# Score products of 64 inputs over all 128 rows, in a two-block transformer on one NeuronCore

## The chip, the cores and the metric

The kernel runs on one core of one Trainium2 chip. The metric is the device time of one execution in microseconds (us). Five engines work side by side: TensorE (PE in the profile, with its weight loads as PEld), VectorE (DVE), ScalarE (ACT), GpSimd (POOL) and SyncE (SP), which mostly issues transfers. Three runs of the kernel before took 2697.49, 2701.44 and 2704.54 us; the median is 2701.44 us.

## The reference, cut to what matters

A first block of two layers works on 512 tokens and a context of 256 tokens, all of width 1024. Each layer modulates and norms its input, projects it, and feeds three mixers: a pooling, a neighbourhood attention of 6 heads, and a bidirectional retention of 6 heads. An output projection and a convolutional FFN follow. A second block (latent attention, a long convolution, a memory attention and 32 experts) comes behind; the change doesn't touch it. All heads of the first block have 64 features, so each score is a sum over 64 inputs:

```python
# neighborhood_attention: each query against a window of 8 rows x 32 columns and 256 context tokens
s_loc = jnp.einsum('bnqhd,binshd->bhnqis', qb, kb)
s_loc = jnp.where(valid, s_loc + bias, NEG_INF)
s_ctx = jnp.einsum('bnqhd,bkhd->bhnqk', qb, kc)
p = jax.nn.softmax(jnp.concatenate([s_loc, s_ctx], axis=-1), axis=-1)
# retention: q and k rotated; the scores times decays instead of a softmax
a = jnp.einsum('bhid,bhjd->bhij', qb, kb) * intra[None]
y = a @ v + (q @ state_of_the_context) * q_dec
```

## The kernel before, in words

**Products.** Every float32 operand is split into two float32r parts, hi and lo, whose sum is exact. A product of 128 inputs (`mm3`) is three matmuls: hi by hi, lo by hi, hi by lo. A score product of 64 inputs (`mm2`) is two. For this, two heads share a tile of 128 partitions, 64 each. One operand (the keys in the attention, the queries in the retention) is stacked: for each head a tile with its hi part in the head's own 64 rows and its lo part in the other 64. The other operand is doubled: its hi part stands on both halves of a tile of each head (`qd`, `rkd`), so the first matmul, over all 128 rows, gives hi by hi and hi by lo. Its lo part stands in one tile for both heads (`ql`, `cql`, `rkl`), and the second matmul takes only the head's own 64 rows of it, `mm(out, xl, ks[r])`.

**Neighbourhood attention** (phase `na_l` of layer l, `neighborhood`). The three pairs of heads come one after the other. A unit is one head's block of 128 queries: 24 units in each layer, and 6 more in layer 0 for the context's own queries (`na_context`). A unit has three stages: scores and softmax, transpose of the probabilities, product with the values. `staged` keeps three units in flight, one stage apart, and the projections of the next pair (`lin`) are woven between them. A unit makes two score products of 256 columns, so two first and two second matmuls.

**Retention** (phase `ret_l`, `ret_pair`), also a pair at a time. The queries are rotated (`rotated`: a shuffled copy `sw`, times a table on POOL, added on DVE), stacked, and multiplied by a decay for either direction (`dq(d)`: an iota on POOL, an exponential on ACT, then a product on POOL into `x`, which is split). The keys are rotated and doubled. `sw`, `x` and the square of the group norm share one buffer, `rsw`; the decays take two, `rd`; the decayed context keys have one, `rckd`. Then each head's blocks of 128 keys go against all 512 queries (four first and four second matmuls for each head, 512 columns wide; in layer 0 the context's 2 blocks as well, 256 columns wide). The scores are multiplied by the decays on DVE, split on ACT and DVE, and multiplied by the values.

A tile scheduler orders the instructions of each engine from the program's order and its own estimates, and a buffer that is asked for again waits until its last reader is done.

Of the kernel before, what the change touches and what calls it, by code (L numbers as in the profile page):

```python
# [11 lines left out]
F32 = mybir.dt.float32  # L12
FR = mybir.dt.float32r
# [5 lines left out]
P = 128  # L19
D = 1024  # L20
KC = D // P
S = 512
# [4 lines left out]
# the FFN's features go through the chip in parts: chunks of 128 in each  # L27
FF = (8, 7, 7)
# adding and taking off MAGIC rounds to the nearest integer
MAGIC = 1.5 * 2.0 ** 23  # L30
# 2 pi in three parts, the first two short enough for exact products with small integers
# [3 lines left out]
# the slots of a tile of an expert's tokens, and the tiles: one for each of the 32 experts, and the  # L35
# most that more tokens than that can take (each 64 of 1024), with one to spare
CAP = 64
# thirds of experts' weights in flight: in memory that gets free before the last linear layer, before
# the routing, and after it
# [3 lines left out]
# the early ones, by the chunk of that layer that they are asked for after  # L43
EARLY = (0, 0, 1, 1, 2, 1, 2, 2)
# experts whose tokens are in flight
GATHERED = 8
# The order of the steps of the four long convolutions (of the first and the second, halves of the channels
# each), and of the output projections of the latent attention and of the hyena.
ON_VECTOR = {(1, 0, 1), (2, 0, 2), (0, 0, 0), (1, 0, 0), (3, 1, 2), (1, 0, 2), (0, 0, 1), (1, 1, 1)}
CONV = "a a a * b a b * * a a a b * a b a * b c c b b b * c b c * d d c c * c d * c d c d d d d d + +".split()  # L50
# The order of the steps that the kernel starts with: of the memory, the filters, the modulation, the stream's loads and
# its norm; and of those left
# [3 lines left out]
# added to the half rows of free slots: beyond the last of the tokens' and the results'  # L56
FREE = 4 * S * 4
# PSUM's banks, by use: linear layers, scores, transposes and statistics, sums over scores, and what
# goes on beside
BANKS = {"lin": 2, "sc": 2, "pt": 2, "o": 1, "bg": 1}  # L60
SL = ((0, S), (S, T))
# the parts that a layer's tokens are taken in where a norm follows: tokens, sequence
SEGS = (((0, S, 0), (S, T, 1)), ((0, C, 0), (C, S, 0)))

# Vectors that the chip takes with their features on the partitions: name, columns.
# [12 lines left out]
# The retention's decays, one column for every pair of heads (64 rows each), and one for each head.  # L78
# [4 lines left out]
def whole(steps):  # L83
    """A generator's result, all its steps taken."""
    while True:
        try:
            next(steps)
        except StopIteration as e:
            return e.value


def weave(main, beside, slots, steps):
    """Both generators' steps: of beside's as large a part as of main's."""
    done = 0
    for i, _ in enumerate(main, 1):
        while done * slots < i * steps:
            next(beside, None)
            done += 1
    whole(beside)
# [6 lines left out]
class Builder:  # L106
    def __init__(self, ctx, tc, a, out):
# [7 lines left out]
        self.opened = {}  # L115
        self.np, self.nw, self.ahead = None, S, 2
        self.turn = True
# [37 lines left out]
    def norms(self, name, width=S, ahead=2, side="right"):  # L155
        """Opens the memory of the norms to come, of no more tokens than width, ahead chunks at a time."""
        self.nw, self.ahead = width, ahead
        self.np, self.np_name = self.open(name, side), name

    def normed(self):  # L160
        """Closes what norms opened."""
# [10 lines left out]

    def weight(self, src, n, pool=None):
        """n columns of 128 rows, split into two float32r parts whose sum is exact."""
# [10 lines left out]
    def exact(self, src):  # L185
        """1024 columns of a constant that comes with its second float32r part."""
# [15 lines left out]
    def doubled(self, tag, n, bufs=2):  # L202
        """Memory for the first operand of mm2: of a pair of heads."""
        return [self.t([P, n], FR, f"{tag}d{i}", bufs) for i in range(2)], self.t([P, n], FR, tag + "l", bufs)

    def split_doubled(self, hd, lo, src, at=lambda t: t):
        """Two heads' src in two parts: the first twice, on both halves of the partitions of a tile of each head."""
        nc = self.nc
        for i in range(2):
            r, o = slice(64 * i, 64 * i + 64), slice(64 - 64 * i, 128 - 64 * i)  # L210
            nc.scalar.copy(at(hd[i][r]), src[r])
            nc.vector.tensor_tensor(out=at(lo[r]), in0=src[r], in1=at(hd[i][r]), op=ALU.subtract)
            nc.scalar.copy(at(hd[i][o]), src[r])  # L213

    def split_stacked(self, out, src, scale):
        """Two heads' src times scale in two parts, on the halves of the partitions of a tile of each head: the
        first in its place, the second on the other half."""
# [7 lines left out]
    def mm2(self, out, xd, xl, ks, r):  # L225
        """mm3 for 64 inputs: a first part on all partitions with both parts at once."""
        mm = self.nc.tensor.matmul
        mm(out, xd, ks, start=True, stop=False)
        mm(out, xl, ks[r], start=False, stop=True)

    def linear_steps(self, w, xh, xl, sl, m=P, ps=None):
        """psum[features, tokens] of one tile of m output features; a step for each 128 inputs."""
# [14 lines left out]
    def linear_turn(self, w, xh, xl, sl):  # L247
        """linear where the scores' banks are free too."""
# [3 lines left out]
    def split(self, hi, lo, src, scale=1.0):  # L252
        """src times a power of two, into two float32r parts."""
# [13 lines left out]
    def rstd(self, acc, count, ones=None):  # L267
        """Of every token, 1 / sqrt(the sum over acc's partitions / count + eps), on each partition. With ones
        [128, m]: of m blocks of partitions."""
# [7 lines left out]
    def tokenwise(self, acc, ones=None):  # L277
        """Memory for something of every token, with the tokens on the partitions: [128, n / 128, m]; and the
        sums over acc's partitions, or over blocks of them."""
# [9 lines left out]
    def spread(self, r, n, bufs=1):  # L289
        """[128 tokens, n / 128, m] -> [128, n], the same on each of m blocks of partitions"""  # L290
# [12 lines left out]
    def add_square(self, acc, ch, first, scale=1.0, tag="sq"):  # L303
        """Adds the square of ch times scale to acc."""
# [8 lines left out]
    def normed_steps(self, h, sl, acc, scale, shift, ah, al):  # L313
        """rmsnorm of h's tokens sl, whose squares' sums by partition are acc, times scale(k) plus shift(k),
        in two parts; a step for the rstd and for each chunk."""
# [11 lines left out]
    def affine_split(self, hi, lo, x, scale, shift=None):  # L327
        """x times the features' scale, plus their shift, in two parts."""
# [20 lines left out]

    def setup(self):  # L350
# [17 lines left out]
        # (norm, layer) -> g * (1 + scale)  # L368
        self.gs = {(l, i): self.const(f"gs{l}{i}", [P, KC, 2]) for l in range(DEPTH) for i in (1, 2)}

    def stream(self):
        """A chunk of features of the residual stream, or of what the mixers return."""
# [5 lines left out]
    def acts(self):  # L378
        """The two parts of 1024 features."""
# [5 lines left out]
    def modulation(self, l, r):  # L385
        """Columns 2048 r to 2048 (r + 1) of silu(c) @ w_mod[l] + b_mod[l], for x and the context."""
# [30 lines left out]
    def modulation_rows(self, l, r, seqs):  # L417
        """The same by products over rows, off the tensor engine, for the sequences seqs. A step for each 128."""
# [27 lines left out]
    def beside(self, *steps):  # L446
        """What goes on beside the rest: a piece at every tick."""
# [18 lines left out]

    def mod_scale(self, l, i, s):
        """The scale and the shift of norm i for sequence s."""
# [3 lines left out]
    def softmax(self, sc, bias=None, groups=1):  # L472
        """Softmax of sc [128 queries, groups * n keys] over the keys of each group."""
# [4 lines left out]
        pr = self.t([P, 512], F32, "pr", 2)[:, :w]  # L478
        sign = 1.0
        if bias is not None:  # L480
            u = self.t([P, 512], F32, "su", 2)[:, :w]
            nc.vector.tensor_tensor_reduce(out=u, in0=sc, in1=bias, scale=-1.0, scalar=3.0e38,
                                           op0=ALU.add, op1=ALU.min, accum_out=small[:, 0:1])
            sc, sign = u, -1.0
# [14 lines left out]
    def transposed(self, pr, ph, pl):  # L499
        """The transpose of pr [128 queries, w keys] in two parts, to ph, pl [128 keys, w / 128, 128 queries]."""  # L500
# [1829 lines left out]
```

## Time and profile before

| | |
|---|---|
| median of 3 runs | 2701.44 us |
| span of the profiled execution | 2694.9 us |
| time outside the span, by the median | 6.5 us |
| neighbourhood attention, layer 0 | 195 to 345 us of the span |
| retention, layer 0 | 345 to 540 us |
| neighbourhood attention, layer 1 | 1211 to 1338 us |
| retention, layer 1 | 1338 to 1506 us |

The span runs from the first to the last instruction of the one profiled execution; the run's time is a few microseconds longer. The four stretches are those in which the changed lines work, 640 us of the span together.

### The profile page before, as it was taken

Reading aid. Unit: us, or ns where it says so; the run is one execution under the profiler, and the core shown is the slowest. Engines: PE = TensorE matmul, PEld = TensorE weight load, DVE = VectorE, ACT = ScalarE, POOL = GpSimd, SP = SyncE. Lnnn points to the kernel's source line nnn. Section 1 sums busy time; section 2 is a strip of 40 time slices with the busy share of each in tenths; the row PEclk is TensorE's granted clock in tenths of the full one; section 3 lists DMA queues with packets and bytes.
Section 4 is the critical chain, followed back from the end, with each engine's and each line's share of the span. In section 5 each row is a group of like instructions: output and inputs, shape, how many; then the busy total and the mean of one; then the engine's idle time right before and its main releaser. Section 6 shows DMA issues by size and latency. Waiting matters only on the chain. (4 is left out here: it accounts for less than half of the span.)

```text
span 2694.9 us, 37557 instructions
## 1 busy us (share of the span) xinstructions
PE 2561.7 (95%) x14286; PEld 2014.3 (75%) x14286; DVE 1713.9 (64%) x2932; ACT 1171.5 (43%) x1971; POOL 421.2 (16%) x432
## 2 busy tenths in 40 slices
PE   7999999999999999989999999999999879989996
PEld 5567767788888888877766888888878768845553
DVE  6656666557667666476666664546788986355554
ACT  6544445655313313354455652434666545311102
POOL 3041111120000000142221200001500540121100
PEclk9999999999999999999999999999999989989998
DMA  7741222152334252252111522233311643689980
GB/s 242 274 153 48 83 87 94 64 162 93 95 121 159 93 187 85 76 170 58 51 40 40 174 94 94 94 102 111 109 63 63 213 135 108 233 309 365 379 324 32
DMA packets 114047, 368.90 MB, mean 137 GB/s; under 512 B 17988, under 2 KB 29648, under 8 KB 101450
## 3 DMA queue, kind: packets, MB, share of 16 engines
q1 hardware_dynamic: 110554, 358.10, 38.6%
q0 software_dynamic: 3312, 8.40, 0.9%
q8 instruction: 113, 1.85, 0.3%
q14 instruction: 68, 0.56, 0.1%
HBM read 356.95 MB, written 13.68 MB: 138 GB/s over the span
## 5 line engine op out<-in xcount | busy, mean ns | idle before, releaser
L198 PE MATMUL lin<-ah,whi 128*128 128x512 f32 (+1 forms) x1504 | 562.4, 374 | 14.3 <-ACT qd L213 9.3
L200 PE MATMUL lin<-al,whi 128*128 128x512 f32 (+1 forms) x1504 | 547.5, 365 | 1.7 <-DVE al L332 1.1
L199 PE MATMUL lin<-ah,wlo 128*128 128x512 f32 (+1 forms) x1504 | 546.1, 364 | 2.8 <-DVE wlo L182 2.8
L181 ACT CAST whi<-wraw 128x1024 fp32r<-128x1024 f32 (+2 forms) x297 | 297.2, 1004 | 305.1 <-PE sc L200 171.0
L182 DVE TENSOR_TENSOR wlo<-wraw,whi 128x1024 fp32r<-128x1024 f32 (+2 forms) x297 | 370.9, 1250 | 91.6 <-ACT whi L181 91.0
L198 PEld LDWEIGHTS lin<-ah,whi 128*128 128x128 f32 x1504 | 286.5, 191 | 70.7 <-ACT qd L213 9.7
L200 PEld LDWEIGHTS lin<-al,whi 128*128 128x128 f32 x1504 | 285.6, 190 | 50.1 <-DVE al L332 2.4
L199 PEld LDWEIGHTS lin<-ah,wlo 128*128 128x128 f32 x1504 | 286.8, 191 | 42.5 <-DVE wlo L182 3.3
L311 POOL TENSOR_TENSOR sqacc<-sqacc,sq 128x256 f32<-128x256 f32 (+1 forms) x101 | 127.3, 1266 | 1087.8 <-ACT sq L310 1086.5
L198 PE MATMUL sc<-ah,whi 128*128 128x256 f32 (+1 forms) x696 | 219.5, 316 | 0.9 <-ACT whi L181 0.9
L199 PE MATMUL sc<-ah,wlo 128*128 128x256 f32 (+1 forms) x696 | 219.1, 315 | 0.0
L200 PE MATMUL sc<-al,whi 128*128 128x256 f32 (+1 forms) x696 | 218.5, 315 | 0.1
L198 PEld LDWEIGHTS sc<-ah,whi 128*128 128x128 f32 x696 | 132.5, 190 | 12.0 <-ACT whi L181 1.1
L199 PEld LDWEIGHTS sc<-ah,wlo 128*128 128x128 f32 x696 | 132.5, 190 | 10.1 <-DVE wlo L182 0.2
L200 PEld LDWEIGHTS sc<-al,whi 128*128 128x128 f32 x696 | 132.2, 190 | 8.4 <-DVE al L257 0.3
L877 DVE SCALAR_TENSOR_TENSOR fv<-lin,vec,fv 128x511 f32<-128x511 f32 x67 | 50.1, 748 | 118.6 <-ACT fv L876 118.5
L1908 PE MATMUL lin<-ew,ex 128*64 128x256 f32 x864 | 116.7, 388 | 0.0
L433 DVE CUSTOM_DVE_ANT_0 mraw<-mraw,crow 128x512 f32<-128x512 f32 x128 | 86.8, 689 | 32.2 <-DMA mraw<-in_w_mod_rows 31.0
L199 PE MATMUL lin<-mh,wlo 128*128 128x512 f32 (+1 forms) x292 | 105.3, 361 | 1.6 <-DVE wlo L182 1.4
L198 PE MATMUL lin<-mh,whi 128*128 128x512 f32 (+1 forms) x292 | 105.3, 361 | 0.0
L200 PE MATMUL lin<-ml,whi 128*128 128x512 f32 (+1 forms) x292 | 104.8, 359 | 0.0
L1908 PEld LDWEIGHTS lin<-ew,ex 128*64 128x64 f32 x864 | 65.7, 138 | 47.0 <-issue 19.6
(633 smaller groups left out, 5339.7 us busy)
## 6 DMA issues: line engine op xcount, KB each, us to landing
ew<-in_w_moe SPq DMA_DIRECT2D x81, 1024.0 KB
wraw<-in_w_up SPq DMA_DIRECT2D x88, 512.0 KB
wraw<-in_w_in SPq DMA_DIRECT2D x61, 512.0 KB
mraw<-in_w_mod SPq DMA_DIRECT2D x48, 512.0 KB
mraw<-in_w_mod_rows SPq DMA_DIRECT2D x96, 256.0 KB
wraw<-in_w_down SPq DMA_DIRECT2D x48, 448.0 KB
wraw<-in_w_out SPq DMA_DIRECT2D x32, 512.0 KB
wraw<-in_w_down SPq DMA_DIRECT2D x16, 512.0 KB
```

The lines of the kernel that those rows point to most:

```text
L181: nc.scalar.copy(hi[:, :n], raw[:, :n])
L182: nc.vector.tensor_tensor(out=lo[:, :n], in0=raw[:, :n], in1=hi[:, :n], op=ALU.subtract)
L198: mm(out, wh, xh, start=start, stop=False)
L199: mm(out, wl, xh, start=False, stop=False)
L200: mm(out, wh, xl, start=False, stop=stop)
L311: nc.gpsimd.tensor_tensor(out=acc, in0=acc, in1=sq, op=ALU.add)
L433: self.tc.keep_in_program_order(nc.vector.tensor_tensor_reduce(out=x, in0=raw, in1=self.crow[:, i, d], scale=1.0, scalar=0.0, op0=ALU.mult ...
L877: nc.vector.scalar_tensor_tensor(out=v[:, t0 + 1:t1], in0=ps[:, :t1 - t0 - 1], scalar=cw(0), in1=v[:, t0 + 1:t1], op0=ALU.mult, op1=ALU.add)
L1908: nc.tensor.matmul(ps[CAP * f:CAP * f + CAP, :256], xk, pieces(512 * k + 256 * f, 256), start=k == 0, stop=k == KC - 1, tile_position=(0, ...
```

## The change

It has three parts. First, the doubled operand's lo part gets a tile for each head, whose other 64 rows are set to zero once a phase, by 16 memsets on POOL in all; the second matmul of `mm2` then runs over all 128 rows, against the whole stacked tile. Second, the softmax of scores with a bias writes biased scores into the buffer of the probabilities, of which there are three in the neighbourhood attention, instead of into a buffer `su` of their own (there were two of each). Third, in the retention `sw`, `x`, the decayed context keys and the square all take the two `rd` buffers, the decays being multiplied in place; `rsw` and `rckd` are gone.

```diff
     def doubled(self, tag, n, bufs=2):
-        return [self.t([P, n], FR, f"{tag}d{i}", bufs) for i in range(2)], self.t([P, n], FR, tag + "l", bufs)
+        key = tag, self.sm.name
+        if key not in self.seconds:
+            self.seconds[key] = []
+            for _ in range(bufs):
+                pair = [self.t([P, n], FR, tag + "l", 2 * bufs) for _ in range(2)]
+                for i, t in enumerate(pair):
+                    self.nc.gpsimd.memset(t[64 - 64 * i:128 - 64 * i].bitcast(F32), 0.0)
+                self.seconds[key].append(pair)
+        lo = self.seconds[key].pop(0)
+        self.seconds[key].append(lo)
+        return [self.t([P, n], FR, f"{tag}d{i}", bufs) for i in range(2)], lo
...
     def split_doubled(self, hd, lo, src, at=lambda t: t):
-            nc.vector.tensor_tensor(out=at(lo[r]), in0=src[r], in1=at(hd[i][r]), op=ALU.subtract)
+            nc.vector.tensor_tensor(out=at(lo[i][r]), in0=src[r], in1=at(hd[i][r]), op=ALU.subtract)
...
-    def mm2(self, out, xd, xl, ks, r):
+    def mm2(self, out, xd, xl, ks):
         mm(out, xd, ks, start=True, stop=False)
-        mm(out, xl, ks[r], start=False, stop=True)
+        mm(out, xl, ks, start=False, stop=True)
...
     def softmax(self, sc, bias=None, groups=1):
-        pr = self.t([P, 512], F32, "pr", 2)[:, :w]
+        pr = self.t([P, 512], F32, "pr", self.probs)[:, :w]
         if bias is not None:
-            u = self.t([P, 512], F32, "su", 2)[:, :w]
-            nc.vector.tensor_tensor_reduce(out=u, in0=sc, in1=bias, scale=-1.0, scalar=3.0e38,
+            nc.vector.tensor_tensor_reduce(out=pr, in0=sc, in1=bias, scale=-1.0, scalar=3.0e38,
-            sc, sign = u, -1.0
+            sc, sign = pr, -1.0
...
     def rotated(self, x):
-        sw = self.t([P, S], F32, "rsw", 1)
+        sw = self.t([P, S], F32, "rd", 2)
...
-            x = self.t([P, S], F32, "rsw", 1)
-            nc.gpsimd.tensor_tensor(out=x, in0=q, in1=dq(d), op=ALU.mult)
+            x = dq(d)
+            nc.gpsimd.tensor_tensor(out=x, in0=q, in1=x, op=ALU.mult)
...
-            kd = self.t([P, C], F32, "rckd", 1)
-            nc.vector.tensor_tensor(out=kd, in0=ck, in1=dk(d), op=ALU.mult)
+            kd = dk(d)
+            nc.vector.tensor_tensor(out=kd, in0=ck, in1=kd, op=ALU.mult)
...
-            sq = self.t([P, S], F32, "rsw", 1)[:, :n]
+            sq = self.t([P, S], F32, "rd", 2)[:, :n]
```

In `layer`, `self.probs` is 3 during the neighbourhood attention and 2 elsewhere. No matmul is added or removed, and PE's order in the neighbourhood attention is the same but for one block. Two places show what moves.

POOL, where the neighbourhood attention of layer 0 begins, before. L838 is the last step of the pooling, `bias` is what is added to the scores of a pair, `vw` a window of the values.

```order
L838 TENSOR_TENSOR hy_1478<-hy_1478,px_1459 128x256
L562 MEMSET bias_1717 128x2x256
L562 MEMSET bias_1798 128x2x256
L844 MEMSET poolw_2348 128x256
L567 TENSOR_TENSOR bias_1717<-bias_1717,namask_1506 128x256 x2
L567 TENSOR_TENSOR bias_1798<-bias_1798,namask_1506 128x256 x2
L570 COPY vw_1729<-vf_1651 128x256
```

The same place of the changed kernel:

```order
L848 TENSOR_TENSOR hy_1478<-hy_1478,px_1459 128x256
L211 MEMSET ql_1567 64x512
L211 MEMSET ql_1568 64x512
L211 MEMSET ql_1571 64x512
L211 MEMSET ql_1572 64x512
L211 MEMSET cql_1583 64x256
L211 MEMSET cql_1584 64x256
L211 MEMSET cql_1587 64x256
L211 MEMSET cql_1588 64x256
L573 MEMSET bias_1731 128x2x256
L573 MEMSET bias_1810 128x2x256
L854 MEMSET poolw_2352 128x256
```

Eight memsets of half a tile stand ahead of the first two biases; layer 1 has four there, and each retention two.

DVE, in the first pair of the retention of layer 0, before. L257 is the second part of a split (here of the decayed queries `rqd0` and `rqd1`), L684 to L687 are the rotation of the keys, L212 the keys' lo part.

```order
L257 TENSOR_TENSOR rqd0l_3532<-rsw_3526,rqd0h_3531 128x512
L737 TENSOR_TENSOR rckd_3704<-rck_3605,rd_3705 128x256
L182 TENSOR_TENSOR wlo_4070<-wraw_4068,whi_4069 128x1024
L257 TENSOR_TENSOR rqd1l_3541<-rsw_3535,rqd1h_3540 128x512
L212 TENSOR_TENSOR rkl_3602<-rck_3605,rkd_3600 64x256
L684 STREAM_SHUFFLE rsw_3667<-rx_3603 128x512
L212 TENSOR_TENSOR rkl_3602<-rck_3605,rkd_3601 64x256
L686 TENSOR_TENSOR rx_3603<-rx_3603,rope_3488 128x512
L687 TENSOR_TENSOR rx_3603<-rx_3603,rsw_3667 128x512
L212 TENSOR_TENSOR rkl_3602<-rx_3603,rkd_3600 64x512
L212 TENSOR_TENSOR rkl_3602<-rx_3603,rkd_3601 64x512
```

The same place of the changed kernel:

```order
L269 TENSOR_TENSOR rqd0l_3517<-rd_3512,rqd0h_3516 128x512
L695 STREAM_SHUFFLE rd_3654<-rx_3590 128x512
L697 TENSOR_TENSOR rx_3590<-rx_3590,rope_3474 128x512
L182 TENSOR_TENSOR wlo_4055<-wraw_4053,whi_4054 128x1024
L269 TENSOR_TENSOR rqd1l_3525<-rd_3520,rqd1h_3524 128x512
L698 TENSOR_TENSOR rx_3590<-rx_3590,rd_3654 128x512
L223 TENSOR_TENSOR rkl_3584<-rck_3592,rkd_3588 64x256
L223 TENSOR_TENSOR rkl_3585<-rck_3592,rkd_3589 64x256
L748 TENSOR_TENSOR rd_3691<-rck_3592,rd_3691 128x256
L223 TENSOR_TENSOR rkl_3584<-rx_3590,rkd_3588 64x512
L223 TENSOR_TENSOR rkl_3585<-rx_3590,rkd_3589 64x512
```

The shuffle of the keys stood behind the split of the second direction, whose buffer it takes; it now stands right behind the split of the first.

## Rows read from the trace of the kernel before

**Rows 1.** The page: the profiled execution's span.
```profile
span 2694.9 us, 37557 instructions
```

**Rows 2.** Windows: length, busy us (count) of PE, PEld, DVE, ACT, POOL; clock; DMA.
```profile
195.00:345.00 150.00, 148.63 (x982) 114.66 (x981) 93.88 (x220) 67.89 (x155) 22.40 (x40) 1.00 0.23 72
345.00:540.00 195.00, 189.66 (x1001) 135.48 (x999) 124.22 (x214) 113.64 (x196) 31.98 (x36) 0.97 0.24 84
1211.00:1338.00 127.00, 123.76 (x823) 99.03 (x823) 80.22 (x183) 59.78 (x123) 24.32 (x37) 1.00 0.18 50
1338.00:1506.00 168.00, 156.05 (x801) 118.86 (x800) 117.87 (x177) 93.15 (x154) 39.28 (x45) 0.97 0.17 58
1358.00:1369.00 11.00, 9.59 (x24) 5.27 (x24) 6.38 (x12) 6.66 (x12) 0.56 (x1) 0.53 0.00 0
371.50:382.20 10.70, 10.70 (x28) 5.55 (x27) 4.86 (x10) 5.96 (x11) 0.56 (x1) 0.52 0.29 98
```

**Rows 3.** One line, L229, the second matmul: count, ns min/median/max, starts, forms.
```profile
L229 PE MATMUL sc<-k,ql x96: 377/382/386, 198.9 to 1330.7; 64*128 64x256 f32 x96
L229 PE MATMUL sc<-rq,rkl x60: 378/497/793, 371.7 to 1482.8; 64*128 64x512 f32 x48, 64*128 64x256 f32 x12
L229 PE MATMUL sc<-k,cql x12: 379/380/382, 235.9 to 339.9; 64*128 64x256 f32 x12
```

**Rows 4.** Timeline of PE around one unit's scores, layer 0: start, us, instruction.
```profile
211.00 0.28 PE L228 MATMUL sc<-k,qd 128*128 128x256 f32 x1
211.21 0.38 PE L229 MATMUL sc<-k,ql 64*128 64x256 f32 x1
211.52 0.38 PE L228 MATMUL sc<-k,qd 128*128 128x256 f32 x1
211.84 0.38 PE L229 MATMUL sc<-k,ql 64*128 64x256 f32 x1
212.14 0.38 PE L198 MATMUL lin<-ah,whi 128*128 128x256 f32 x1
212.37 0.28 PE L199 MATMUL lin<-ah,wlo 128*128 128x256 f32 x1
```

**Rows 5.** Timeline of PE in a projection, 256 columns, five pitches apart.
```profile
1353.66 0.28 PE L200 MATMUL lin<-al,whi 128*128 128x256 f32 x1
...
1354.26 0.28 PE L199 MATMUL lin<-ah,wlo 128*128 128x256 f32 x1
```

**Rows 6.** Timeline of PE in the retention of layer 0.
```profile
386.33 0.45 PE L228 MATMUL sc<-rq,rkd 128*128 128x512 f32 x1
386.70 0.49 PE L229 MATMUL sc<-rq,rkl 64*128 64x512 f32 x1
387.13 0.50 PE L200 MATMUL lin<-al,whi 128*128 128x512 f32 x1
387.46 0.39 PE L198 MATMUL lin<-ah,whi 128*128 128x512 f32 x1
387.69 0.39 PE L199 MATMUL lin<-ah,wlo 128*128 128x512 f32 x1
```

**Rows 7.** Timeline of POOL as the neighbourhood attention of layer 0 begins.
```profile
186.66 0.99 POOL L562 MEMSET bias<- 128x512 f32 x2
187.59 0.31 POOL L844 MEMSET poolw<- 128x256 f32 x1
...
192.58 1.58 POOL L567 TENSOR_TENSOR bias<-bias,namask 128x256 f32<-128x256 f32 x2 [3.27 <-DMA bias<-in_rpb]
```

**Rows 8.** PE's waits, 345 to 540 us: waiting line, releaser: us, times, longest.
```profile
PE pt L265 <- ACT ry L717: 3.9, 1, 3.9
```

**Rows 9.** PE's waits, 1338 to 1506 us.
```profile
PE sc L228 <- ACT rkd L213: 3.5, 1, 3.5
```

**Rows 10.** Timeline of POOL at the start of the retention of layer 1.
```profile
1351.63 1.41 POOL L704 TENSOR_TENSOR rsw<-rx,rd 128x512 f32<-128x512 f32 x1 [1.04 <-DVE rqd0l L257]
```

**Rows 11.** Timeline of DVE at the same place.
```profile
1354.77 0.72 DVE L684 STREAM_SHUFFLE rsw<-rx 128x512 f32<-128x512 f32 x1
```

More of the change, by code (lines that the diff above doesn't have):

```diff
@@ L114, in __init__ @@
         self.background = iter(())
-        self.opened = {}
+        self.opened, self.seconds = {}, {}
         self.np, self.nw, self.ahead = None, S, 2
-        self.turn = True
+        self.turn, self.probs = True, 2
         self.meanwhile = iter(())
@@ L573, in na_unit @@
         sc = self.psum("sc")
-        self.mm2(view(sc[:, :256], "p (r w) -> p r w", w=32), qd[i][:, q], ql[r, q], window(k[:, :S]), r)
-        self.mm2(sc[:, 256:], qd[i][:, q], ql[r, q], k[:, S:], r)
+        self.mm2(view(sc[:, :256], "p (r w) -> p r w", w=32), qd[i][:, q], ql[i][:, q], window(k[:, :S]))
+        self.mm2(sc[:, 256:], qd[i][:, q], ql[i][:, q], k[:, S:])
         pr = self.softmax(sc, at["bias"][:, i])
@@ L595, in na_context @@
             q = slice(j * P, j * P + P)
-            self.mm2(sc[:, j * C:j * C + C], qd[i][:, q], ql[r, q], k[:, S:], r)
+            self.mm2(sc[:, j * C:j * C + C], qd[i][:, q], ql[i][:, q], k[:, S:])
         pr = self.softmax(sc, groups=2)
@@ L762, in ret_pair @@
                 self.tick(2)
-                r = slice(64 * i, 64 * i + 64)
                 for j in range(n // P):
@@ L766, in ret_pair @@
                     kc = slice(t0 + j * P, t0 + j * P + P)
-                    self.mm2(sc, k2[i][:, kc], kl[r, kc], qs[i][:, t0:t1], r)
+                    self.mm2(sc, k2[i][:, kc], kl[i][:, kc], qs[i][:, t0:t1])
                     x = self.t([P, S], F32, "rx", 2)[:, :n]
@@ L980, in layer @@
                 y[2 + p] = self.stream()
+            self.probs = 3
             self.neighborhood(l, ah, al, need_ctx, y)
+            self.probs = 2
         with self.phase(f"ret_{l}"):
```

## The prediction

> **What bounds the kernel now.** First the page, for the span: 2694.9 us [rows 1]. The run's median is 6.5 us above it; I make the sum against the span and add the 6.5 at the end. Then the windows, to see who is busy in the four stretches in which the changed lines work [rows 2]. The reader is to see that PE has hardly a gap in the neighbourhood attention: 148.63 of 150 us in layer 0, 123.76 of 127 in layer 1, at full granted clock. DVE is busy for 93.88 and 80.22 us, about 63% of each. In the retention PE has 189.66 of 195 and 156.05 of 168 us, DVE 124.22 and 117.87, which is 64% and 70%. So PE sets the pace in all four, and a microsecond that its stream loses is a microsecond of the kernel as long as the softmax and the splits of the others keep up.
>
> A busy PE needn't be an efficient one, though, so the third view is the timeline of PE, read by its pitch, the time from one start to the next. In a projection five pitches of 256 columns take 1354.26 - 1353.66 = 0.60 us, 0.12 each [rows 5]. Around a unit's scores the same width takes much longer: from the first score product to the second product behind the last there are five pitches in 212.37 - 211.00 = 1.37 us [rows 4]. Each start around a 64-row product comes 0.21 to 0.32 us after the one before, going into it and coming out of it. In the retention, with 512 columns, three pitches take 387.46 - 386.33 = 1.13 us where the next one takes 387.69 - 387.46 = 0.23 [rows 6]. So a 64-row product costs its own extra time and that of the change from 128 rows to 64 and back.
>
> The Trainium skill, "TensorEngine Tiling (Array Packing)", Key Properties, says that changing the tiling mode drains TensorE. If the 64-row product counts as such a mode, the slow pitches are the drain, and the trace agrees (0.31 against 0.12 us).
>
> **The change, part by part.**
>
> *All 128 rows.* How often: the line of the second product stands 96 + 12 times in the neighbourhood attention and 60 times in the retention, 48 of them 512 columns wide and 12 with 256 [rows 3]. In the neighbourhood attention that makes 54 units of two. The changed product has the shape of the first one, and with it every product of the stream has 128 rows, so I price it at the pitch of the projection: a unit gets 1.37 - 0.60 = 0.77 us back, 54 x 0.77 = 41.6 us. In the retention a wide one gets 1.13 - 3 x 0.23 = 0.44 us back, 48 x 0.44 = 21.1 us, and a narrow one half a unit's share, 0.39 us, 12 x 0.39 = 4.7 us. Together 67.4 us. That is the upper end for this part. The lower end is nothing, if what slows the pitch were not the rows but the operand (the k tile, the window's stride of the moving data); the first product reads the same k tile over 128 rows, and the retention's operands have no stride and show the same slow pitch, so I take the upper end as the freed PE time.
>
> Not all of it reaches the end. In the neighbourhood attention PE would need about 23 us less in layer 0 (30 units x 0.77) and 18 us less in layer 1 (24 x 0.77). DVE's share rises to 93.88 / 127 and 80.22 / 108.5, 74% in both. That is below the bound, but the three stages of a unit pass from PE to DVE to ACT and back, and in the last pair no projections of a next attention pair fill the gaps. I take a sixth off, 7 us (the ends: nothing, and a half). In the retention PE already idles for 195 - 189.66 = 5.3 and 168 - 156.05 = 12 us, that is where chains over other engines end last. I take a third off, 8.6 us (the ends: nothing, and two thirds). What is left: 41.6 - 7 + 25.8 - 8.6 = 51.8 us.
>
> *The memsets.* The trace has no 64-row memset on POOL. Above: a memset of 128x512 takes 0.99 / 2 = 0.5 us, one of 128x256 takes 0.31 [rows 7]. At the start of layer 0 four and four come ahead of the bias, 4 x 0.5 + 4 x 0.31 = 3.2 us at most. The second bias's addition there waits 3.27 us for its transfer [rows 7], so they fit: 0. Below nothing they can't go, since no engine's work is taken away for them. Without that cover they would cost those 3.2 us, and 2 us (four) in layer 1. In the retention two of 64x768 stand at the head of each pair's first phase only, at most 2 x 0.75 us by the same rate, and the trace shows PE in projections then: 0. What stands behind them on POOL is the bias, and behind that the windows of the values `vw`; the first probabilities would wait.
>
> *The softmax in place.* The same instructions; three buffers where two and two were. A unit holds its buffer from the scores to the transpose, and at most two stages of it are alive at a time, so the third one is spare: 0. If it were not, PE's idle time of 1.4 and 3.2 us in these windows [rows 2] would grow; that is part of the sixth above.
>
> *The shared retention buffers.* This moves the rotation of the keys. Before, the shuffle (DVE L684) takes `rsw` after both directions of the decayed queries are split; in layer 1 it starts at 1354.77 [rows 11]. The second direction's multiplication starts at 1351.63, as soon as the first's split is done [rows 10]. With two buffers the shuffle needs only that first split, so it can start up to 1354.77 - 1351.63 = 3.1 us earlier. At its end stands the doubled key, for which PE waits 3.5 us there [rows 9]. In layer 0 the 3.9 us wait is for the values' copy [rows 8], which doesn't hang on that buffer. So the gain is 3.1 us once, and the lower end is a loss: the second direction's iota and exponential now come behind the queries' rotation, whose buffer they take. That chain, where it is late, delays the states of the context and not the scores. I take 3 us gained, between -5 and +6.5 (both waits).
>
> **The sum.** 51.8 + 3 = 54.8 us. Span 2694.9 - 54.8 = 2640, and with the 6.5 us outside it 2646 us.
>
> **The rivals.**
>
> *The chain takes over.* Freed of the drains, PE waits in each unit for the softmax of the unit before, and more than half of the gain is gone. For it: DVE at 74% with a chain of several steps per unit. Against it: hardly any waiting now, 1.4 us in 150 [rows 2]. With 45% of 67.4 us left, 2701.4 - 30 = 2671 us.
>
> *The half clock goes too.* After the waits of rows 8 and 9 the granted clock is 0.52 and 0.53 over 10.7 and 11.0 us [rows 2], the lower of its two levels (1.2 of 2.4 GHz). In such a stretch PE does half of its work, so the two cost up to 10.7 x 0.48 + 11.0 x 0.47 = 10.3 us. If the gap ahead of them gets shorter and the clock stays, the time is 2646 - 10 = 2636, and with no loss in the neighbourhood attention 2629 us. For it: the earlier keys in layer 1. Against it: layer 0's wait stays, and a faster PE reaches the gap sooner.
>
> *Row count is nothing.* The pitch stays as it was and the time stays at 2701 us. Against it: the first product, with 128 rows, does run at 0.12 us where only 128-row products surround it [rows 5]. The Trainium skill, "TensorE: Matmul & The Clock Gate", Why this matters for your kernels, says that a product of few rows takes the time of one of 128; by it alone the padding would give nothing. The slow pitches of rows 4 and 6 disagree.
>
> *Slower: the two shared buffers serialise the retention.* The copy `sw`, both directions, the context keys and the square now pass through two buffers. If every handover had to be waited for, one costs a multiplication of 1.41 us, its wait of 1.04 [rows 10] and an operation like the shuffle, 0.72 [rows 11]: 3.2 us, four a pair, six pairs, 76 us: 2646 + 76 = 2722 us. It decides from 54.8 / 6 = 9.1 us a pair on, three of the four handovers exposed. Against it: `x` had one buffer before and has two now, and only 3.5 us of exposed wait stand in all of this window at the place concerned [rows 9].
>
> **How the numbers follow.** The forecast, drains gone with a part lost to chains (2630 to 2660 us): 0.60. The chain takes over (2660 to 2685): 0.16. The half clock goes too (2615 to 2636): 0.17. Row count is nothing (2701): 0.04. Serialised retention (2722): 0.03. The predicted time is the likeliest's, 2646 us. The range of 2620 to 2672 us holds the forecast, most of the half-clock case and half of the case of chains; it leaves out the last two, the upper half of the second, and a little below, together under 0.2. A measurement of this kernel tells about 0.3% (8 us) from no change; faster than that are the first three cases, 0.93, the same 0.04, slower 0.03.
>
> **What would show it.** Right: the pitch around the second products of a unit at 0.12 us, five in some 0.6 us; both attention windows shorter by 15 to 20 us each; the memsets at the start of POOL's work with the bias's addition where it was; the shuffle of the keys behind the first split and the 3.5 us wait below 1 us. Wrong: a slow pitch that stays, then the rows were not the cause; PE waits of over 10 us in a window for the transposes (the chain took over); waits for `rd` in the retention (serialised); a granted clock below 0.9 in the attention, which now has it at 1.00, would take back what the pitch gives.

## The result, and the profile after

The changed kernel takes 2655.68 us (median; 2654.33 to 2657.90), beside 2701.95 us for the kernel before: ratio 0.9832, 95% interval 0.9818 to 0.9846, or 46 us less. The forecast was 2646 us, 55 us less. The profiled execution is a run of 2654.92 us, near the median. The one of before was among the shorter ones: in every later execution with both figures the time exceeds the span by only 1.7 to 1.9 us, so most of the 6.5 us that the forecast added was not time outside the span. The two spans therefore differ by less than the medians: by 41.8 us. One execution of a later kernel (the values in `rah`) took 3507.36 us at a granted clock of 0.65, and it is left out of that kernel's figures.

The page of the changed kernel, for its span:

```profile
span 2653.1 us, 37574 instructions
```

The timeline of PE around one unit's scores, the place of [rows 4]:

```profile
209.29 0.28 PE L240 MATMUL sc<-k,qd 128*128 128x256 f32 x1
209.41 0.28 PE L241 MATMUL sc<-k,ql 128*128 128x256 f32 x1
209.53 0.28 PE L240 MATMUL sc<-k,qd 128*128 128x256 f32 x1
209.65 0.28 PE L241 MATMUL sc<-k,ql 128*128 128x256 f32 x1
209.77 0.28 PE L198 MATMUL lin<-ah,whi 128*128 128x256 f32 x1
209.89 0.28 PE L199 MATMUL lin<-ah,wlo 128*128 128x256 f32 x1
```

The same five pitches now take 209.89 - 209.29 = 0.60 us, not 1.37. The second product is as fast as its neighbours. The others changed too, as the view by line says (the columns are those of [rows 3]):

```profile
L241 PE MATMUL sc<-k,ql x96: 278/282/467, 198.8 to 1294.9; 128*128 128x256 f32 x96
L241 PE MATMUL sc<-rq,rkl x60: 274/395/775, 354.0 to 1439.4; 128*128 128x512 f32 x48, 128*128 128x256 f32 x12
```

What came of it by stretch? The windows of [rows 2] hold different work in a faster kernel, so the next two fences go from the first score of a mixer to its last, which is the same work in both. First the kernel before: attention and retention of layer 0, then of layer 1.

```profile
198.70:339.60 140.90, 140.75 (x921) 107.66 (x919) 90.11 (x209) 65.10 (x148) 20.32 (x34) 1.00 0.22 68
371.30:529.90 158.60, 157.25 (x803) 110.45 (x803) 98.00 (x172) 90.23 (x157) 22.35 (x27) 0.97 0.24 83
1219.60:1330.30 110.70, 109.24 (x728) 86.78 (x726) 72.78 (x169) 53.39 (x112) 22.19 (x33) 1.00 0.18 51
1359.40:1482.50 123.10, 117.83 (x548) 85.93 (x548) 82.78 (x129) 66.94 (x113) 23.51 (x27) 0.96 0.12 39
```

And the changed kernel, with one window more for its clock:

```profile
198.70:321.30 122.60, 119.59 (x921) 101.29 (x920) 88.67 (x209) 64.15 (x146) 22.39 (x37) 1.00 0.29 89
353.70:508.10 154.40, 149.86 (x805) 108.28 (x805) 99.29 (x171) 90.67 (x158) 23.61 (x28) 0.99 0.26 86
1196.90:1294.80 97.90, 95.56 (x728) 84.01 (x727) 71.23 (x169) 52.84 (x112) 22.73 (x33) 0.97 0.21 60
1323.60:1439.20 115.60, 109.07 (x546) 85.24 (x547) 84.05 (x130) 68.45 (x116) 23.68 (x28) 0.97 0.14 43
1286.20:1293.00 6.80, 6.21 (x39) 5.69 (x38) 3.71 (x9) 1.54 (x3) 0.00 (x0) 0.50 0.00 0
```

The attention lost 18.3 and 12.8 us of its length, the retention 4.2 and 7.5. PE, which had 0.2 us free in the first stretch, now has 3.0, and DVE is at 72% and 73%, as forecast. In layer 1 a piece of 6.8 us of the attention runs at the lower clock, which it did not before. A second trace of the same kernel (the change again, below) doesn't show this piece: there the attention of layer 1 takes 95.2 us at a clock of 1.00 and the retention 114.8 us at 0.99. So some 3 us of a stretch can differ between two executions of one kernel.

The memsets stand where the order had them (POOL, start of layer 0):

```profile
187.08 2.21 POOL L211 MEMSET ql<- 64x512 f32 x4
189.33 1.36 POOL L211 MEMSET cql<- 64x256 f32 x4
...
193.07 1.43 POOL L578 TENSOR_TENSOR bias<-bias,namask 128x256 f32<-128x256 f32 x2 [1.19 <-DMA bias<-in_rpb]
```

They take 3.6 us, and the bias's addition still waits 1.19 us for its transfer: covered.

### The profile page after: what moved, and what is told of

It is laid out like the page before. It is cut to its first block, busy times and chain, and to the rows that moved or that the text cites. A ratio compares the mean times of both kernels' runs of the same rounds, so it can differ in the third digit from the quotient of the medians.

```text
span 2653.1 us, 37574 instructions
## 1 busy us (share of the span) xinstructions
PE 2511.2 (95%) x14286; PEld 2005.6 (76%) x14286; DVE 1711.6 (65%) x2932; ACT 1171.2 (44%) x1971; POOL 432.8 (16%) x448
## 5 line engine op out<-in xcount | busy, mean ns | idle before, releaser
L182 DVE TENSOR_TENSOR wlo<-wraw,whi 128x1024 fp32r<-128x1024 f32 (+2 forms) x297 | 362.7, 1223 | 85.3 <-ACT whi L181 83.6
L1920 PEld LDWEIGHTS lin<-ew,ex 128*64 128x64 f32 x864 | 65.2, 136 | 46.3 <-issue 18.3
```

Of the source, the lines that this page charges most:

```text
L182: nc.vector.tensor_tensor(out=lo[:, :n], in0=raw[:, :n], in1=hi[:, :n], op=ALU.subtract)
L1920: nc.tensor.matmul(ps[CAP * f:CAP * f + CAP, :256], xk, pieces(512 * k + 256 * f, 256), start=k == 0, stop=k == KC - 1, tile_position=(0, ...
```

## The experiments

**The rows alone, in three kernels.** They keep the changed kernel's tiles, memsets, buffers and PE order, and only the rows of the second product differ: 64 everywhere, 64 in the retention, 64 in the attention.

```diff
-    def mm2(self, out, xd, xl, ks):
+    def mm2(self, out, xd, xl, ks, r=slice(None)):
-        mm(out, xl, ks, start=False, stop=True)
+        mm(out, xl[r], ks[r], start=False, stop=True)
...
-        self.mm2(sc[:, 256:], qd[i][:, q], ql[i][:, q], k[:, S:])
+        self.mm2(sc[:, 256:], qd[i][:, q], ql[i][:, q], k[:, S:], r)
```

Expected of 64 rows everywhere:

> The changed kernel with all its tiles, memsets and buffers, but the second score product over the head's own 64 rows again, in the same order on PE. If the rows alone gave the gain (theory), it loses the whole 46 us: 2695 to 2705 us, the same as the kernel before. If the shared buffers and the earlier rotation of the keys gave the retention's part of about 12 us (rival), it stays at 2685 to 2692 us. If the memsets cost something, it is above 2705 us.

Of 64 rows in the retention only:

> As the changed kernel, with 64 rows in the retention's second products only. Theory (every second product has its price there too, the forecast's 17 us after losses, or the 8 to 12 us that the two traces differ by there): 2664 to 2672 us. Rival (the retention's part comes from the buffers, not from the rows): 2654 to 2659 us.

Of 64 rows in the attention only:

> As the changed kernel, with 64 rows in the neighbourhood attention's second products only. Theory (31 us lie in the two attention stretches, all of it by the rows): 2683 to 2690 us. Rival (a part of it comes from the probabilities' three buffers): 2670 to 2680 us.

| second products | median us | ratio to before, interval |
|---|---|---|
| 64 rows everywhere | 2705.11 | 1.0008 (0.9998 to 1.0017) |
| 128 in the attention only | 2673.40 | 0.9894 (0.9877 to 0.9910) |
| 128 in the retention only | 2688.91 | 0.9953 (0.9937 to 0.9970) |
| 128 everywhere (the change) | 2655.68 | 0.9832 (0.9818 to 0.9846) |

PE's order is the same, product for product, in these three and the changed kernel. Everything but the rows makes no difference that can be told. With 128 rows in the attention only, the time is 1.4 us above the range expected; with 128 in the retention only it is inside its range, and with 64 everywhere at the upper edge. The rows in the attention are worth 31.7 us without those of the retention and 33.2 with them; the rows in the retention 16.2 and 17.7. The two add up. So the retention's part does not come from the buffers, as one rival had it, and the memsets cost nothing to be seen.

The stretches of the kernel with 64 rows everywhere show where the two traces misled:

```profile
374.90:539.60 164.70, 161.19 (x804) 109.61 (x803) 99.77 (x171) 90.74 (x158) 23.59 (x28) 0.98 0.25 80
...
1368.40:1490.30 121.90, 117.07 (x547) 85.77 (x547) 84.66 (x131) 68.47 (x116) 24.56 (x28) 0.96 0.13 41
```

Its retention of layer 0 takes 164.7 us where that of the kernel before takes 158.6. The rows took 10.3 us from 164.7, and the two traces alone show 4.2. The new order of the retention costs some 6 us there and gives 1.2 in layer 1; by the medians, what isn't the rows costs 1.5 us (by the interval from -0.5 to +4.6). Its profiled run was its slowest, 2707.61 us, but two more traces agree: the stretch takes 165.6 us with 128 rows in the attention only, and 159.3 us in the next experiment, which has the order of before.

Most of the 6 us lies in products that the prediction doesn't mention: 70 products with the modulation weights (`bg`), which are woven into this stretch. Their part of the windows, before and with 64 rows everywhere, and two of their groups in the second kernel:

```profile
371.30:529.90 158.60, 13.25 (x70) 1.19 (x70) 0.97 0.24 83
374.90:539.60 164.70, 18.31 (x70) 1.59 (x70) 0.98 0.25 80
```

```profile
428.86 1.04 PE L407 MATMUL bg<-mraw,csil 128*2 128x512 f32 x8
445.03 1.02 PE L407 MATMUL bg<-mraw,csil 128*2 128x512 f32 x2
```

A group of two takes as long as one of eight. The order of before has the 70 in 12 groups, the new order in 17, and PE is busy with them for 5.1 us more. Which part of the change moved them was not tested.

**Change of rows, or the 64 rows themselves?** In the kernel before, the second half of a unit's scores takes its 64-row product first, so that the unit's two stand side by side.

```diff
-        self.mm2(sc[:, 256:], qd[i][:, q], ql[r, q], k[:, S:], r)
+        mm = self.nc.tensor.matmul
+        mm(sc[:, 256:], ql[r, q], k[r, S:], start=True, stop=False)
+        mm(sc[:, 256:], qd[i][:, q], k[:, S:], start=False, stop=True)
```

> The kernel before, with the two products of the second half of a unit's scores in the other order (64 rows first, then 128), so that the unit's two 64-row products stand side by side: two changes between 128 and 64 rows a unit instead of four, in 48 units. If the price is that of the change between 128 and 64 rows (theory), half of 0.77 us goes, 48 x 0.385 = 18 us: 2680 to 2688 us. If it is the price of a 64-row product itself (rival), nothing changes: 2698 to 2704 us.

It took 2692.36 us, ratio 0.9960 (0.9945 to 0.9974). The timeline of PE around a unit's scores in this kernel:

```profile
210.55 0.28 PE L228 MATMUL sc<-k,qd 128*128 128x256 f32 x1
210.76 0.39 PE L229 MATMUL sc<-k,ql 64*128 64x256 f32 x1
210.99 0.28 PE L576 MATMUL sc<-k,ql 64*128 64x256 f32 x1
211.20 0.39 PE L577 MATMUL sc<-k,qd 128*128 128x256 f32 x1
211.42 0.28 PE L198 MATMUL lin<-ah,whi 128*128 128x256 f32 x1
211.54 0.29 PE L199 MATMUL lin<-ah,wlo 128*128 128x256 f32 x1
```

Five pitches take 0.99 us: 0.39 more than without any 64-row product, where four changes cost 0.77. There are as many 64-row products in these units as before and half as many changes, and the price is half: about 0.19 us a change. That is the theory; the rival is out. If 64 rows count as a tiling mode of their own, which no run here shows, the Trainium skill's rule that a change of mode drains TensorE ("TensorEngine Tiling (Array Packing)", Key Properties) agrees with these 0.19 us. The Trainium skill's sentence that a product of few rows (it names 32) takes as long as one of 128 ("TensorE: Matmul & The Clock Gate", Why this matters for your kernels) leaves that price out.

The traces also show what PE does in those 0.19 us. Each product needs a weight load (PEld). Here are the loads of the second, third and fourth product of the fence above, then one of the kernel before [rows 4] and one of the changed kernel:

```profile
210.76 0.18 PEld L229 LDWEIGHTS sc<-k,ql 64*128 64x128 f32 x1
210.87 0.19 PEld L576 LDWEIGHTS sc<-k,ql 64*128 64x128 f32 x1
211.20 0.19 PEld L577 LDWEIGHTS sc<-k,qd 128*128 128x128 f32 x1
...
211.21 0.18 PEld L229 LDWEIGHTS sc<-k,ql 64*128 64x128 f32 x1
...
209.29 0.19 PEld L241 LDWEIGHTS sc<-k,ql 128*128 128x128 f32 x1
```

Where the row count stays, the load starts 0.12 us ahead of its product (210.87 for 210.99, 209.29 for 209.41) and runs beside the product before. Where the row count changes, in either direction, it starts only with its own product (210.76, 211.20, 211.21), and its 0.18 to 0.19 us are not covered: as much as a change costs. It is so at each of the 336 changes around the 168 second products of the kernel before. Why the load is not started earlier there, no trace says.

The time fell short of 2680 to 2688 us, though. The windows, first score to last, of attention and retention:

```profile
199.40:331.90 132.50, 132.34 (x923) 104.71 (x921) 89.36 (x210) 65.07 (x148) 20.28 (x34) 1.00 0.26 73
...
1212.50:1314.30 101.80, 100.42 (x728) 83.79 (x727) 71.36 (x167) 52.05 (x110) 23.86 (x33) 1.00 0.21 55
1344.90:1476.90 132.00, 126.78 (x548) 91.89 (x548) 83.00 (x130) 67.13 (x113) 23.50 (x27) 0.89 0.12 36
```

The attention gave 8.4 and 8.9 us, 17.3 of the 18 expected. In this execution the retention of layer 1 took 8.9 us more: 132.0 us at a mean clock of 0.89, not 123.1 at 0.96. Its start is at the lower clock for 20.5 us, where before it was 11.0 us [rows 2], after the same wait of 3.5 us:

```profile
1344.90:1365.40 20.50, 20.50 (x50) 13.02 (x51) 8.79 (x18) 6.50 (x15) 0.63 (x2) 0.51 0.09 26
```

The five times go with the clock: 2686.51 us at a mean of 0.978, inside the range expected, and 2689.54 to 2694.27 us at 0.973 to 0.975. So the missing part goes with time at the lower clock. That the freed time upstream caused it is not shown.

**Where the rest of the freed time went.** Four kernels, each the changed kernel with one edit. The keys' projection and rotation ahead of the two decays:

```diff
+        ps = self.project(l, 14 + p, ah, al, (0, 1))
+        k2, kl = self.doubled("rk", T, 1)
...
+        self.split_doubled(k2, kl, self.rotated(kx), lambda t: t[:, :S])
...
         qd = []
         for d in range(2):
...
-        ps = self.project(l, 14 + p, ah, al, (0, 1))
-        k2, kl = self.doubled("rk", T, 1)
...
-        self.split_doubled(k2, kl, self.rotated(kx), lambda t: t[:, :S])
```

> The changed kernel with the keys' projection and rotation written ahead of the queries' two decays. Theory (the earlier shuffle of the keys gave nothing because its last addition on DVE stood behind a weight's split of 2.30 us and the second direction's split of 0.68 us, and PE still waits 3.5 us there and then has the lower clock for some microseconds): the wait falls by about 3 us in each layer and a part of the lower clock's 3.4 us goes: 2648 to 2653 us. Rival (the decayed queries or the context's states are then late instead): 2654 to 2660 us.

The probabilities of the scores with a bias divided on ACT:

```diff
-            nc.vector.tensor_scalar(out=pr[:, c], in0=pr[:, c], scalar1=small[:, 4 + g:5 + g],
-                                    scalar2=None, op0=ALU.mult)
+            if bias is None:
+                nc.vector.tensor_scalar(out=pr[:, c], in0=pr[:, c], scalar1=small[:, 4 + g:5 + g],
+                                        scalar2=None, op0=ALU.mult)
+            else:
+                nc.scalar.activation(out=pr[:, c], in_=pr[:, c], func=AF.Copy, scale=small[:, 4 + g:5 + g])
```

> The changed kernel with the division of the biased probabilities on ACT instead of DVE, 48 instructions of about 0.5 us each. Theory (what the neighbourhood attention lost of the freed PE time goes to waits on DVE's part of the softmax): DVE falls from 70% to under 60% there and the time by 3 to 8 us, 2648 to 2653 us. Rival (the chain's length counts and not DVE's share, and on ACT it is no shorter): 2654 to 2660 us.

Four units in flight (`vt`, the transposed values, is then made in the added stage):

```diff
+        pr = self.softmax(sc, at["bias"][:, i])
+        yield
+        if i == 0:
             vw = self.t([P, 256], F32, "vw", 2)
...
         pr = self.softmax(sc, groups=2)
         yield
+        yield
...
-            live = [unit] + live[:2]
+            live = [unit] + live[:depth]
```

> The changed kernel with four units of the neighbourhood attention in flight instead of three: a whole stage lies between a unit's softmax and its transpose. Theory (PE's new waits are the length of the chain from scores to transpose): they vanish, 3 to 7 us less in the two attention stretches, 2649 to 2653 us. Rival (the longer run-out at the end of each pair costs as much): 2654 to 2660 us.

And more work for DVE:

```diff
+        if bias is not None:
+            nc.vector.tensor_scalar(out=pr, in0=pr, scalar1=1.0, scalar2=None, op0=ALU.mult)
         return pr
```

> The changed kernel with a second, idle scaling (by 1.0) of each unit's probabilities on DVE, 48 of about 0.5 us, 24 us of DVE work. If DVE's chain now sets the pace in the attention (the rival of the prediction), most of it is seen: 2668 to 2680 us. If PE still does and the chain has slack in most units (theory), a third or less: 2658 to 2664 us.

| edit to the changed kernel | median us | ratio to before, interval |
|---|---|---|
| keys first | 2649.88 | 0.9804 (0.9784 to 0.9825) |
| division on ACT | 2653.08 | 0.9817 (0.9796 to 0.9838) |
| four units in flight | 2649.93 | 0.9804 (0.9783 to 0.9825) |
| more DVE | 2663.90 | 0.9858 (0.9834 to 0.9881) |

By the times alone only more DVE stands apart from the change: all five of its runs (2660.80 to 2670.52 us) lie above all nine of the change and its repeat (2648.43 to 2657.90 us). The traces say a little more. More DVE adds 48 x 0.48 = 23 us of work and 8.2 us of time: DVE is near the pace of the attention without setting it.

With four units in flight the last score stands further ahead of the last product, so first score to last is no longer the same work. The next windows go from the first score of the attention to the first of the retention. First the change, then the change again (layer 1 only), then four units:

```profile
198.70:353.70 155.00, 145.88 (x1080) 121.18 (x1079) 115.30 (x250) 82.48 (x182) 35.42 (x52) 1.00 0.29 91
1196.90:1323.60 126.70, 118.15 (x881) 103.51 (x879) 92.42 (x201) 65.36 (x133) 37.60 (x50) 0.97 0.20 58
...
1201.50:1325.10 123.60, 115.56 (x880) 100.82 (x878) 94.10 (x201) 65.35 (x133) 36.73 (x50) 1.00 0.20 57
...
195.60:347.50 151.90, 143.79 (x1074) 121.52 (x1073) 115.73 (x250) 82.44 (x182) 35.83 (x52) 0.99 0.30 90
1191.50:1314.60 123.10, 115.40 (x880) 101.18 (x878) 93.68 (x201) 66.28 (x133) 33.84 (x49) 1.00 0.21 57
```

Layer 0 is shorter by 3.1 us, and by 2.7 against the change again (154.6 us). That much of the chain's length was exposed there. Layer 1 is shorter by 3.6 us, but by only 0.5 against the change again, whose trace has no spell at the lower clock either; so no gain is shown there. The division on ACT, which takes DVE to 64% and 63% and not under 60%, gave 1.2 and 0.9 us, first score to last, too little to tell.

Why did the earlier shuffle of the keys give nothing? The DVE timeline of the changed kernel at the retention of layer 1, the place of [rows 11]:

```profile
1316.30 0.69 DVE L269 TENSOR_TENSOR rqd0l<-rd,rqd0h 128x512 fp32r<-128x512 f32 x1 [1.84 <-ACT rqd0h L268]
...
1317.04 0.75 DVE L695 STREAM_SHUFFLE rd<-rx 128x512 f32<-128x512 f32 x1
1317.82 1.00 DVE L697 TENSOR_TENSOR rx<-rx,rope 128x512 f32<-128x512 f32 x1
1318.74 2.30 DVE L182 TENSOR_TENSOR wlo<-wraw,whi 128x1024 fp32r<-128x1024 f32 x1
1320.97 0.68 DVE L269 TENSOR_TENSOR rqd1l<-rd,rqd1h 128x512 fp32r<-128x512 f32 x1
1321.57 0.68 DVE L698 TENSOR_TENSOR rx<-rx,rd 128x512 f32<-128x512 f32 x1
```

The shuffle does stand right behind the first split. But DVE then takes a weight's split and the second direction's split ahead of the rotation's last addition, and PE's wait for the doubled key is what it was (3.5 us, [rows 9]):

```profile
PE sc L240 <- ACT rkd L224: 3.5, 1, 3.5
```

With the keys first that wait is gone, but PE waits 3.3 us for the copy of the values instead; the retention's stretches are shorter by 2.1 and 3.5 us.

**Together.** Four more kernels: the change again, the two edits together, then also the values' copy in another buffer (`rah` for `rx`), and last that copy ahead of the decays too.

```diff
-        v = [self.t([P, S], F32, *tag) for tag in (("rx", 2), ("ry", 1))]
+        v = [self.t([P, S], FR, "rah", 2).bitcast(F32), self.t([P, S], F32, "ry", 1)]
```

> The changed kernel once more, unaltered, beside the next two on the same chip: 2653 to 2658 us by every theory. It shows what differences between these kernels can be told.

> The changed kernel with the keys ahead of the decays and with four units in flight in the attention. Each alone gave 5.8 us. If they act in different stretches (theory): 2642 to 2646 us. If both only moved the same wait and the same lower clock at the start of the retention (rival): 2648 to 2651 us.

> The same, with the copy of the retention's values in a buffer of the split scores (rah) instead of that of the rotated queries (rx), which it has to wait for with the keys first: PE waited 3.0 and 3.3 us for that copy. Theory (that wait is exposed in both layers): 3 to 6 us below the kernel with both alone. Rival (the buffer of the split scores is then late for the pairs behind the first): the same or slower.

> The kernel of the run before (keys first, four units in flight, values in rah) with the values' copies written ahead of the two decays too. There the wait stayed though the buffer was free, because the copy stood on ACT behind a weight's cast and the second direction's split, and PE's queue had the values' transposes ahead of the first score. Theory: with the copies ahead the wait of 3.3 to 3.8 us falls under 1 us in both layers, and the time to 2637 to 2642 us. Rival (the decayed queries or the context's states are late next): 2643 to 2648 us.

| kernel | median us | ratio to before, interval |
|---|---|---|
| the change again | 2654.74 | 0.9813 (0.9792 to 0.9835) |
| keys first, four units | 2644.41 | 0.9787 (0.9768 to 0.9806) |
| and values in `rah` | 2646.13 | 0.9786 (0.9767 to 0.9806) |
| and values ahead | 2639.20 | 0.9777 (0.9761 to 0.9792) |

The two edits together are 10.3 us below the change again, and neither undoes the other: the first score of the attention to that of the retention takes 151.9 us in layer 0, as with four units, and the two stretches of the retention, first score to last, take 151.9 and 112.6 us, about as with the keys first (152.3 and 112.1). The buffer was not what the values waited for, so the third did nothing and its theory falls. ACT's timeline of that kernel, layer 1, shows what it was:

```profile
1313.90 0.72 ACT L679 ACTIVATE rd<-rd,vec 128x512 f32<-128x512 f32 x1
1314.53 1.03 ACT L181 CAST whi<-wraw 128x1024 fp32r<-128x1024 f32 x1
1316.16 0.62 ACT L268 CAST rqd1h<-rd 128x512 fp32r<-128x512 f32 x1 [0.61 <-POOL rd L727]
1316.69 0.58 ACT L734 COPY rah<-lin 128x512 f32<-128x512 f32 x1
```

The copy stands behind a weight's cast and the second direction's split on ACT's own queue. With the copy ahead of the decays, the last kernel takes 2639.20 us, as expected, but not for the reason expected. PE's wait for the copy only fell to 2.1 to 2.7 us and not under 1, and the wait for the second copy (`ry`) grew instead; in layer 1:

```profile
PE pt L277 <- ACT ry L728: 4.5, 3, 2.0
PE pt L277 <- ACT rah L728: 2.1, 1, 2.1
```

Its two stretches of the retention are as long as those of the kernel before it (151.7 and 112.7 us beside 151.8 and 112.8). Of the 7.1 us by which the two spans differ, 4.1 lie ahead of the first score of the attention (197.0 us beside 201.1), where the edit does nothing; over all traces here that first score comes between 195.6 and 202.0 us. So the 5 to 7 us below the two kernels before it are not shown to come from the edit, and that the forecast was met is luck. It is the fastest version here, 16 us below the change.

## Why the prediction was right, point by point

- *All 128 rows, attention.* Forecast 41.6 us freed and 34.6 after a sixth was taken off; measured 31.7 to 33.2. The pitch of 0.60 us for five came out to the digit. The loss was a fifth to a quarter. Of the two windows that were to be 15 to 20 us shorter, layer 0 is (18.3 us); layer 1 is not (12.8 us, and 15.5 in the change again).
- *All 128 rows, retention.* Forecast 25.8 freed and 17.2 after a third; measured 16.2 to 17.7. The agreement is in part luck. Compared place by place, the changed kernel and the one with 64 rows differ by about 0.39 us a product at either width, the price of two changes; the forecast had 0.44 for the wide ones. That makes some 23 us freed, and a loss of a quarter to three tenths of it.
- *The losses* were put down to chains over other engines. In the attention one more unit in flight brought back some 3 us in layer 0, and extra DVE work showed to a third. In the retention no experiment tests it. That row count itself is nothing, the rival at 2701 us, is out by the three kernels with 64 rows.
- *The memsets and the softmax in place* at 0: with the shared buffers they come to 1.5 us together, not told from 0.
- *The shared retention buffers* at +3 us is the term that failed. The shuffle came earlier as forecast, and nothing came of it, because the addition at the end of the rotation waits in DVE's queue; the wait of 3.5 us, which was to fall below 1 us, stayed. I had followed the buffer and not the queue behind it. Nor had I looked at what else the new order moves: in layer 0 the modulation products, in five more groups, take 5.1 us more. Measured with the two zeros above, 1.5 us lost: some 4.5 us of the 8.5 by which 54.8 exceeds 46.3. Another 1.4 to 2.9 is the attention's; the rest is within the interval of the ratio (4 us either way).
- *The half clock* did not go as a whole. In the first trace of the changed kernel the retention of layer 1 is at 0.97 (before 0.96) and the attention of layer 1, new, at 0.97; in the second they are at 0.99 and 1.00. Layer 0's retention has 0.99 in both, from 0.97. The spells differ between executions of one kernel, so no part of the 46 us is shown to come from them.
- *Serialised retention* did not come: the largest wait of PE in that stretch is the old one of 3.5 us.

## What to carry to other kernels

Read PE by its pitch as well as by its busy share: a stream that looks 99% busy paid 0.19 us at every change between 128-row and 64-row products, and zero-filled rows, which do no useful work, removed it. The weight loads show the place: look for loads that start with their own product and not beside the one before. Where the shape can't be changed, put the odd products side by side. When a transfer of buffers lets a step start earlier, follow the step's last instruction through its engine's queue before the gain is counted, and compare how the rest of the stream is grouped.

## What the runs showed of the hardware that was not expected

The price of a 64-row product follows the number of changes and not of products: 0.77 us for four changes, 0.39 for two, nothing for none. It equals the 0.18 to 0.19 us of a weight load, which at a change starts only with its own product; between two 64-row products side by side the load runs ahead again. The price is the same, about 0.39 us for two changes, with 256 and with 512 columns.

The length of a spell at the lower clock varies from execution to execution. With the adjacent products, a retention with unchanged work ran at a mean clock of 0.89 where it had 0.96 and took 8.9 us longer, after the same wait of PE. The runs don't show why.
